# Five buffers instead of two for staged weights, and squares counted by section, in a two-layer attention kernel

## The chip, the cores and the metric

The kernel runs on one core of one Trainium2 chip. The metric is device time in microseconds (us) of that core; lower is better. The core's engines work side by side, each through its own list of instructions in a fixed order: PE multiplies matrices (PEld is its weight load), DVE, ACT and POOL do elementwise work, and SP issues the DMA transfers. An instruction that waits holds everything behind it on its own engine. An engine's order is not the order of the text: the build plans it, and may put an instruction ahead of others that stand before it in the text when what it needs is expected to be there.

## What is computed

A trunk of two layers on x of 1024 rows and 1024 columns, all float32. Each layer computes

```
x <- x + W_out( mixer(RMSNorm(x)) * silu(z) )
```

where q, k, v and z of the mixer come from one combined input projection of the normed x, and a last RMSNorm follows. Layer 0's mixer is "FoX", causal attention of 16 heads of 64 with a forget gate:

```python
logits = jnp.einsum('bqhd,bkhd->bhqk', q[:, s0:s1], k[:, :s1]) * scale
logits = logits + c[:, :, s0:s1, None] - c[:, :, None, :s1]     # c: running sum of log forget gates
logits = jnp.where(tk[None, :] <= tq[:, None], logits, NEG)
p = jax.nn.softmax(logits, axis=-1)
outs.append(jnp.einsum('bhqk,bkhd->bqhd', p, v[:, :s1]))
```

Layer 1's mixer is "NSA": 16 query heads in 4 groups attend in three ways, to 63 compressed blocks of keys, to 8 chosen blocks of 64 keys, and to a window of 512 keys; the three results are summed with sigmoid gates. The projections of both layers, and both output projections, are what the weights of this case are for.

## The kernel before, in words

**Weights come in sections.** The columns of the input projections are cut into sections of 128 columns, each 1024 x 128 float32, 512 KB in DRAM and 4 KB in each of the 128 partitions of on-chip memory. FoX has 32 of them (k, v, q and z for each of 8 pairs of heads, `p`), NSA has 28 (kc, vc, qa, qr, v, ka, kr, z). Rows of W_out, 8 for each layer, are brought in the same shape so that their sum of squares is known in advance; they are called `wor`.

**Life of a section.** `Staged` (L163) takes a place of the tag `wst`, of which there are two, and issues the transfer on SP (L169). `square` (L172) sums the squares of the section on ACT (L176, into `wj`, the sum in `wsq`) and `total` copies the sum for the next step on ACT (L133, `wsb`, three places). `split` (L180) spreads the sum over the partitions with a small matmul on PE (L138, `wsum`), makes a power of two of it on DVE, and writes the section as two float16 halves, `whi` on DVE (L190) and `wlo` in four pieces on POOL (L193 and L194). With the last `wlo` piece the section's `wst` place is free. A `wor` has no split: its place is free after its square.

**How far ahead.** `next_w` (L347 for FoX, L929 for NSA) is called where a section begins. It keeps two sections split, so the next one is split while this one is used, and then `stage_next` begins the transfer of the one after that, if none is staged. The squares wait in a list; `flush` (L159) runs all of them, and `project` (L213), the loop of 24 matmuls of one half of a section, calls it after its fifth step. `wo_square` (L366) stages one `wor` beside each pair of heads in FoX, and beside eight of NSA's sections.

**What runs beside it.** `merge` weaves two streams: for FoX the attention of head pairs (`FoxDuo`, scores, softmax and the product with v) with the projections of the next pair (`fox_fill`); for NSA first the compressed attention (`cmp_main`), then the attention of the 32 head halves (`NsaSuper`), with projections and the output projection as filling. Around a section's use ACT and DVE also copy its product out: K (L433, L434), v (L508, L509), Q (L530, L531) and z (L85, L86).

**Others with the same tag.** `OutPart` (L578) loads parts of the attention output into a `wst` place for the output projection, and `load_wout` (L678) loads W_out rows through `wst` places and converts them (L695 to L700). Both are in the stretch in which a layer's output projection runs. `load_wout` with `half` set first adds up the `wor` squares.

Of the kernel before, what the change touches and what calls it, by code (L numbers as in the profile page):

```python
# [8 lines left out]
F32 = mybir.dt.float32  # L9
# [12 lines left out]
P = 128  # L22
H = 16
HD = 64
KC = D // P
# [16 lines left out]
def tile_fox_nsa(ctx, tc, a, out):  # L42
# [36 lines left out]
    wp = ctx.enter_context(tc.tile_pool(name="wp", bufs=2))  # L79
# [8 lines left out]
    class Norm:  # L88


        def __init__(self, pool, x, name, bufs):
            self.x, self.n = x, 0
            self.st = pool.tile([P, 4], F32, tag="st", bufs=bufs, name=f"st_{name}")
            self.h = pool.tile([P, D], F32, tag="h", bufs=bufs, name=f"h_{name}")
# [19 lines left out]
    def to_hT(h, t, hT, name, ps=(ps_t, ps_t)):  # L114
        for c in range(2):
            pt = ps[c](f"pth_{name}_{c}")
            for j in range(4):
                T.transpose(pt[:, j * P:(j + 1) * P], h[:, (4 * c + j) * P:(4 * c + j + 1) * P], ident)
            hi = hT[t // 4][0][:, 4 * c:4 * c + 4, t % 4 * P:(t % 4 + 1) * P]
            lo = hT[t // 4][1][:, 4 * c:4 * c + 4, t % 4 * P:(t % 4 + 1) * P]  # L120
            v = pt.rearrange("p (k t) -> p k t", k=4)
            A.copy(hi, v)
            V.tensor_tensor(lo, v, hi, OP.subtract)
# [7 lines left out]
    def total(sq, name, ps):  # L131
        sb = wp.tile([P, 2], BF16, tag="wsb", bufs=3, name=f"wsb_{name}")
        A.copy(sb, sq.to_broadcast([P, 2]))  # L133
        return lambda: spread(sb, name, ps)
# [21 lines left out]
    gains = []  # L156
    squares = []

    def flush():  # L159
        while squares:  # L160
            squares.pop(0)()

    class Staged:  # L163


        def __init__(self, src, name, acc=None):
            self.name, self.acc, self.sq = name, acc, None
            self.st = wp.tile([P, KC, P], F32, tag="wst", bufs=2, name=f"wst_{name}")
            dma(self.st, src)  # L169
            squares.append(self.square)  # L170

        def square(self):  # L172
            if self.sq is None:
# [23 lines left out]
    def weight_scale(pt, u, undo):  # L197

        b, e, r, x = (u[:, i:i + 1] for i in range(4))
        exponent(pt, r, b)  # L200
        V.tensor_scalar(r, r, 2.0 ** 77, None, OP.mult)
        if undo is None:
            V.tensor_scalar(e, b, 2.0 ** 50, None, OP.mult)
        else:
            V.tensor_scalar(e, b, undo, 2.0 ** 50, OP.mult, OP.mult)
        return e, r, x
# [6 lines left out]
    def project(w, hT, half, pt):  # L213
        for k in range(KC):
            mm3(pt, w[0][:, k, :], w[1][:, k, :], hT[half][0][:, k, :], hT[half][1][:, k, :], k == 0, k == KC - 1)
            if k == 4:
                flush()
            yield 650
# [121 lines left out]
    st = tc.alloc_tile_pool(name="start", bufs=1, side="right")  # L340
# [3 lines left out]
    fox_order = [x for p in range(8) for x in ((1, p), (2, p), (0, p), (3, p))][1:]  # L344
    wq, staged = [], []

    def next_w():  # L347
        while len(wq) < 2 and (staged or fox_order):
            if not staged:
                stage_next()  # L350
            wq.append(staged.pop(0).split(gains[0].undo))
        stage_next()
        return wq.pop(0)

    def stage_next():
        if not staged and fox_order:
            kind, p = fox_order.pop(0)
            staged.append(Staged(a["fox_w"][kind * 8 + p], f"{'qkvz'[kind]}{p}"))

# [3 lines left out]
    def w_row(i, k):  # L363
        return w_out[i][k * P:(k + 1) * P, :].rearrange("p (k c) -> p k c", k=KC)
# [75 lines left out]
    def opening():  # L440
        gB = st.tile([P, D], F32, name="gB")
        xs = []
        for i in range(2):
            gains.append(Gain(a["norm_g_c"][:, i * KC:(i + 1) * KC], i))
        for t in range(NT):
            xs.append(st.tile([P, D], F32, tag="x", bufs=7, name=f"x_{t}"))
            dma(xs[t], a["x"][t * P:(t + 1) * P, :])
            if t == 0:
                dma(gB, a["norm_g"][0:1, :].to_broadcast([P, D]))
            if t == 1:  # L450
                k0w = Staged(a["fox_w"][8], "k0")
            if t == 3:
                dma(wfst, a["fox_w_f"].rearrange("(k p) c -> p k c", p=P))
                dma(bf[32:32 + H], a["fox_b_f"].rearrange("o h -> h o"))
                dma(below, a["below"])
        dma(tri, a["tri"])
        side = []
        hs = {}
        with tc.manual_schedule(engines={T.engine, V.engine, A.engine}):
            for t in range(NT + 1):  # L460
                if t < NT:
                    nm = Norm(st, xs[t], f"n0_{t}", 3)
                    nm.square(slice(0, D))
                    hs[t] = nm.finish(gB, gain=gains[0])
                if t:
                    to_hT(hs.pop(t - 1), t - 1, hT, f"n0_{t - 1}", (ps_s, ps_t))
                if t == 2:
                    flush()
                if t == 3:
                    wq.append(k0w.split(gains[0].undo))  # L470
                    A.activation(fj, wfst, AF.Square, accum_out=fsq)
                    fsum = total(fsq, "f", ps_t)
                if t == 4:
                    e, r, _ = weight_scale(fsum(), fu, gains[0].undo)
                    wfe.append(e)
                    V.tensor_scalar(wf[:, :, 0:H], wfst, r, None, OP.mult)
                    V.scalar_tensor_tensor(wf[:, :, 32:32 + H], wfst, r, wf[:, :, 0:H], OP.mult, OP.subtract)
                    side = [k0] * 9 + [gate0] * 8
                if t >= 5:
                    for g in side[0:5]:  # L480
                        next(g)
                    del side[0:5]
            for g in side:
                next(g)

    k0, gate0 = fox_k(0), forget_gate()
    opening()

    def v_transposes(vt, half, vT, name):
# [88 lines left out]
    class OutPart:  # L578


        def __init__(self, i, t, k0, stop):
            self.name, self.i, self.t, self.k0, self.stop = f"{i}_{t}_{k0}", i, t, k0, stop
            self.of = wp.tile([P, KC, P], F32, tag="wst", bufs=2, name=f"of{self.name}")[:, k0:stop, :]
            dma(self.of, oF[k0 * P:stop * P, t * P:(t + 1) * P].rearrange("(k p) t -> p k t", p=P))

        def square(self):
# [91 lines left out]
    def load_wout(pool, i, half):  # L678

        if half:  # L680
            u = consts.tile([P, 6], F32, name=f"wou{i}")
            V.tensor_reduce(u[:, 4:5], sqW[i], AX.X, OP.add)
            wout_undo[i], r, _ = weight_scale(total(u[:, 4:5], f"wo{i}", ps_t)(), u, None)
            wout_scale[i] = r
        r = wout_scale[i]
        hi, lo = (pool.tile([P, 4, D], F16, tag=f"h{half}{x}", name=f"wo{i}_{half}_{x}") for x in range(2))
        yield 0
        for k in range(4):
            st = wp.tile([P, KC, P], F32, tag="wst", bufs=2, name=f"wor{i}_{half}_{k}")
            dma(st, w_row(i, 4 * (1 - half) + k))  # L690
            st = st.rearrange("p k c -> p (k c)")
            for c in range(2):
                yield 400 if i else 200
                cs = slice(c * 512, c * 512 + 512)
                A.activation(hi[:, k, cs], st[:, cs], AF.Copy, scale=r)  # L695
                if c:
                    V.scalar_tensor_tensor(lo[:, k, cs], st[:, cs], r, hi[:, k, cs], OP.mult, OP.subtract)
                else:
                    G.tensor_scalar(st[:, cs], st[:, cs], r, 1.0, OP.mult, OP.mult)
                    G.tensor_tensor(lo[:, k, cs], st[:, cs], hi[:, k, cs], OP.subtract)  # L700
        ready.setdefault("wout", []).append((hi, lo))
# [220 lines left out]
    nq, wq, squared = list(nsa_w), [], list(range(KC))  # L922

    def stage_next():
        if not staged and nq:
            kind, i = nq.pop(0)
            staged.append(((kind, i), Staged(a["nsa_w"][nsa_i[kind] + i], f"n{kind}{i}")))

    def next_w(key):  # L929
        while len(wq) < 2 and (staged or nq):  # L930
            stage_next()
            k, st = staged.pop(0)
            wq.append((k, st.split(gains[1].undo)))
        stage_next()
        k, w = wq.pop(0)
        assert k == key
        return w
# [222 lines left out]
    gwe, r, _ = weight_scale(total(gu[:, 4:5], "g", ps_t)(), gu, gains[1].undo)  # L1160
# [550 lines left out]
```

## Time and profile before

| | |
|---|---|
| three runs | 1683.37, 1693.61, 1690.54 us; median 1690.54 us |
| the profiled execution | 1687.15 us, of which the span of the instructions is 1685.4 us |
| instructions | 30876 |
| DMA | 237.44 MB in 406558 packets, 141 GB/s on average |
| DVE busy | 1126.5 us, 67% of the span |
| POOL busy | 734.6 us, 44% of the span |
| squares of staged weights (L176) | 76 on ACT, 1.06 us each, with a read of the sum of 0.19 us |
| transfers of staged weights (L169) | 76, in FoX from 3.5 us to 547.6 us, in NSA from 691.8 us to 1327.7 us |

Read in time, the span has these stages: the opening, in which x is normed (0 to about 62 us); FoX (62 to about 580 us); the end of layer 0 with its output projection and the norm for layer 1 (580 to about 750 us); NSA's projections and compressed attention (750 to about 1140 us); NSA's attention with the z projections as filling (1140 to about 1605 us); the end. The profile counts an engine as idle before an instruction and names what ended the idle time; PEclk is the granted clock of PE as a share of full speed.

### The profile page before, as it was taken

What the parts mean: (1) busy time and instruction counts of PE and PEld (TensorE: products, weight loads), DVE (VectorE), ACT (ScalarE), POOL (GpSimd) and SP (SyncE); (2) the same over time, 40 slices, a digit from 0 to 9 for tenths busy, and PEclk for the clock granted to TensorE, in tenths of its full rate; (3) what the DMA queues carried; (4) which work ended last, traced back from release to release, by engine and by line L of the source; (5) the groups of instructions that cost most, each with busy time, mean ns of one, the idle gap of its engine ahead of it and who ended that gap; (6) DMA issues with size and microseconds to landing.
All of it is one profiled execution on the core that took longest, in us unless ns stands there. A gap on an engine that the chain in (4) does not pass through costs nothing. (4 is left out here: it accounts for less than half of the span.)

```text
span 1685.4 us, 30876 instructions
## 1 busy us (share of the span) xinstructions
PE 1425.8 (85%) x10581; PEld 840.7 (50%) x10581; DVE 1126.5 (67%) x3223; ACT 943.1 (56%) x2353; POOL 734.6 (44%) x1057
## 2 busy tenths in 40 slices
PE   5898988988788877958988787887999999989887
PEld 3344444444344433434534444445777777857633
DVE  6486677785767778383724355856787788868754
ACT  6375556655555556254323356656676667766642
POOL 1354334344334431023533334535666676765600
PEclk9899999999899997969989999999999999999999
DMA  6355566766566677251343447756678686776632
GB/s 213 92 137 135 136 134 139 160 124 146 115 136 126 169 169 141 69 186 50 112 129 112 153 125 177 177 167 165 143 143 161 135 189 152 163 172 147 125 111 100
DMA packets 406558, 237.44 MB, mean 141 GB/s; under 512 B 332352, under 2 KB 356544, under 8 KB 406400
## 3 DMA queue, kind: packets, MB, share of 16 engines
q1 hardware_dynamic: 406400, 235.47, 58.2%
q8 instruction: 83, 1.36, 0.4%
q14 instruction: 75, 0.61, 0.1%
HBM read 120.32 MB, written 35.19 MB: 92 GB/s over the span
## 5 line engine op out<-in xcount | busy, mean ns | idle before, releaser
L1481 ACT ACTIVATE P_n<-P_n,m_n 128x640 f32<-128x640 f32 (+7 forms) x256 | 186.7, 730 | 50.7 <-DVE m_n L1480 26.2
L1471 PE MATMUL S_n<-nk,nq 128*128 128x320 f32 (+5 forms) x768 | 194.5, 367 | 13.7 <-DVE m_n L1478 11.9
L782 ACT ACTIVATE P<-P,m 128x512 f32<-128x512 f32 (+1 forms) x192 | 116.4, 607 | 83.9 <-DVE m L773 83.8
L784 DVE SCALAR_TENSOR_TENSOR hl<-P,hl 128x512 f16<-128x512 f32 (+1 forms) x192 | 116.6, 623 | 48.4 <-ACT hl L783 47.3
L1485 POOL TENSOR_TENSOR hl_n<-P_n,hl_n 128x640 f16<-128x640 f32 (+4 forms) x128 | 141.9, 1109 | 8.9
L1471 PEld LDWEIGHTS S_n<-nk,nq 128*128 128x128 f32 x768 | 127.4, 194 | 32.6 <-DVE m_n L1478 18.4
L1484 POOL CAST hl_n<-P_n 128x640 f16<-128x640 f32 (+4 forms) x128 | 76.8, 600 | 130.9 <-ACT P_n L1481 127.9
L753 POOL TENSOR_TENSOR Bd<-B,tri 128x128 f32<-128x128 f32 x128 | 62.7, 504 | 155.8 <-DVE m L773 147.2
L229 DVE SCALAR_TENSOR_TENSOR ptl_n<-ptp_n,pth_n 128x512 f16<-128x512 f32 (+1 forms) x160 | 100.2, 633 | 38.5 <-ACT pth_n L228 37.0
L1478 DVE CUSTOM_DVE_ANT_0 P_n<-S_n,wmask 128x640 f32<-128x640 f32 (+2 forms) x192 | 112.8, 595 | 17.1 <-PE S_n L1471 14.0
L228 ACT ACTIVATE pth_n<-ptp_n 128x512 f16<-128x512 f32 (+1 forms) x160 | 86.1, 544 | 40.7 <-PE ptp_n L1503 38.6
L209 PE MATMUL y<-wo,ohi 128*128 128x512 f16 x230 | 90.4, 393 | 11.8 <-ACT ohi L598 9.2
L1503 PE MATMUL ptp_n<-ident,P_n 128*128 128x128 f32 x576 | 92.1, 281 | 8.5 <-DVE ptl_n L229 4.3
L764 PE MATMUL S<-K,Q 128*128 128x512 f16 (+1 forms) x192 | 62.3, 342 | 42.3 <-DVE m L773 26.9
L783 ACT ACTIVATE hl<-P 128x512 f16<-128x512 f32 (+1 forms) x192 | 92.2, 511 | 4.7 <-DMA pT<-hl 3.3
L211 PE MATMUL y<-wo,olo 128*128 128x512 f16 x230 | 88.6, 389 | 1.4 <-DVE olo L599 1.2
L210 PE MATMUL y<-wo,ohi 128*128 128x512 f16 x230 | 89.7, 390 | 0.0
L1511 PE MATMUL O_n<-nv,pth_n 128*128 128x64 f16 x576 | 71.8, 195 | 13.9 <-ACT pth_n L228 13.9
L1503 PEld LDWEIGHTS ptp_n<-ident,P_n 128*128 128x128 f32 x576 | 66.7, 142 | 25.7 <-DVE ptl_n L229 12.5
L1478 DVE CUSTOM_DVE_ANT_0 P_n<-S_n,bias 128x640 f32<-128x640 f32 (+1 forms) x64 | 65.1, 1018 | 12.4 <-PE S_n L1471 12.0
L798 PE MATMUL O<-v,pT 128*128 128x128 f16 x576 | 60.2, 224 | 13.6 <-DMA pT<-hl 12.1
L1512 PE MATMUL O_n<-nv,pth_n 128*128 128x64 f16 x576 | 71.2, 194 | 0.0
(557 smaller groups left out, 4659.9 us busy)
## 6 DMA issues: line engine op xcount, KB each, us to landing
nq<-qD SPq DMA_DIRECT2D x64, 256.0 KB
B<-cD SPq DMA_DIRECT2D x16, 512.0 KB
nq<-qD SPq DMA_DIRECT2D x64, 128.0 KB
x<-in_x_dram SPq DMA_DIRECT2D x8, 512.0 KB
wst_k<-in_fox_w_dram SPq DMA_DIRECT2D x8, 512.0 KB
wst_v<-in_fox_w_dram SPq DMA_DIRECT2D x8, 512.0 KB
xr<-in_x_dram SPq DMA_DIRECT2D x8, 512.0 KB
wst_q<-in_fox_w_dram SPq DMA_DIRECT2D x8, 512.0 KB
```

The lines of the kernel that those rows point to most:

```text
L209: T.matmul(ps, wh, mh, start=first, stop=False, **kw)
L210: T.matmul(ps, wh, ml, start=False, stop=False, **kw)
L211: T.matmul(ps, wl, mh, start=False, stop=last, **kw)
L229: V.scalar_tensor_tensor(lo[:, 0:n], pt[:, 0:n], scale, h, OP.mult, OP.subtract)
L782: A.activation(L[:, 0:n], L[:, 0:n], AF.Exp, bias=init, scale=-1.0, accum_out=self.lr[:, col + c:col + c + 1])
L783: A.activation(hi[:, cs], L[:, 0:n], AF.Copy, scale=UP)
L784: V.scalar_tensor_tensor(lo[:, cs], L[:, 0:n], UP, hi[:, cs], OP.mult, OP.subtract)
L1471: T.matmul(ps[:, b, 0:w], self.q[x][:, qi * P:(qi + 1) * P], k[:, k0 + b * w:k0 + b * w + w], start=(x == 0), stop=(x == 1))
L1478: V.tensor_tensor_reduce(dst, src, mk, 1.0, 3e38, OP.add, OP.min, m)
L1481: A.activation(L, L, AF.Exp, bias=m, scale=-1.0, accum_out=self.l[:, y, qi:qi + 1])
L1485: G.tensor_tensor(hl[:, n:2 * n], L, hl[:, 0:n], OP.subtract)
L1503: T.transpose(pt[:, (x + i) * P:(x + i + 1) * P], L[:, kb * P - k0:(kb + 1) * P - k0], ident)
```

## The change

The tag `wst` gets five places instead of two wherever it is used. `next_w` now keeps two sections staged behind the two split ones, so that in the text a section's transfer is issued three sections before its use and not two. Each entry in the list of squares carries the number of the section in which it was staged (`now`), and `flush` runs those that are at least one section old; a new call `flush(0)` in `load_wout` and the one in the opening run all. For a section the square stands at the same place of the text as before, while its transfer stands one section earlier. A `wor` of NSA has its square one section later in the text than before.

```diff
+    now = [0]
+
+    def flush(age=1):
+        while squares and squares[0][0] + age <= now[0]:
+            squares.pop(0)[1]()
-    def flush():
-        while squares:
-            squares.pop(0)()
...
-            self.st = wp.tile([P, KC, P], F32, tag="wst", bufs=2, name=f"wst_{name}")
+            self.st = wp.tile([P, KC, P], F32, tag="wst", bufs=5, name=f"wst_{name}")
             dma(self.st, src)
-            squares.append(self.square)
+            squares.append((now[0], self.square))
...
     def next_w():
+        now[0] += 1
         while len(wq) < 2 and (staged or fox_order):
             if not staged:
                 stage_next()
             wq.append(staged.pop(0).split(gains[0].undo))
-        stage_next()
+        while len(staged) < 2 and fox_order:
+            stage_next()
         return wq.pop(0)
 
     def stage_next():
-        if not staged and fox_order:
+        if fox_order:
...
                 if t == 2:
-                    flush()
+                    flush(0)
...
-            self.of = wp.tile([P, KC, P], F32, tag="wst", bufs=2, name=f"of{self.name}")[:, k0:stop, :]
+            self.of = wp.tile([P, KC, P], F32, tag="wst", bufs=5, name=f"of{self.name}")[:, k0:stop, :]
...
     def load_wout(pool, i, half):
 
         if half:
+            flush(0)
...
-            st = wp.tile([P, KC, P], F32, tag="wst", bufs=2, name=f"wor{i}_{half}_{k}")
+            st = wp.tile([P, KC, P], F32, tag="wst", bufs=5, name=f"wor{i}_{half}_{k}")
...
     def stage_next():
-        if not staged and nq:
+        if nq:
...
     def next_w(key):
+        now[0] += 1
         while len(wq) < 2 and (staged or nq):
-            stage_next()
+            if not staged:
+                stage_next()
             k, st = staged.pop(0)
             wq.append((k, st.split(gains[1].undo)))
-        stage_next()
+        while len(staged) < 2 and nq:
+            stage_next()
```

## The prediction

> **What bounds the kernel now.** I first read the clock and the busy times: on average PE bounds the kernel, and ACT, which has the squares, is busy about half of the time.
>
> ```profile
> core 0: 1685.4 us, clock 0.938
> PE 1425.8 (85%) x10581; PEld 840.7 (50%) x10581; DVE 1126.5 (67%) x3223; ACT 943.1 (56%) x2353; POOL 734.6 (44%) x1057
> ```
>
> A share over the whole span says little, so next the table by stage (length, then busy time of PE, PEld, DVE, ACT, POOL, then the granted clock). These are FoX and the start of NSA.
>
> ```profile
> core 0: us, PE busy (x) PEld busy (x) DVE busy (x) ACT busy (x) POOL busy (x), PEclk, DMA share, GB/s
> 62.00:580.00 518.00, 442.81 (x2774) 221.74 (x2772) 364.69 (x1192) 296.22 (x725) 219.15 (x364) 0.95 0.61 138
> 690.00:780.00 90.00, 71.76 (x319) 35.32 (x317) 51.46 (x112) 37.58 (x88) 19.57 (x32) 0.81 0.35 116
> ```
>
> In FoX PE is idle for 518 - 443 = 75 us, and no other engine is near full. So I asked for what ACT waits in FoX; the list names ACT's line, what ended the wait, the sum, the count and the longest.
>
> ```profile
> ACT wj_z L176 <- DMA wst_z<-in_fox_w_dram: 36.8, 8, 7.1
> ACT wj_v L176 <- DMA wst_v<-in_fox_w_dram: 34.1, 7, 6.8
> ACT wj_wor L176 <- DMA wst_wor<-in_fox_w_out_dram: 17.3, 6, 6.4
> ACT wj_k L176 <- DMA wst_k<-in_fox_w_dram: 11.1, 5, 3.6
> ACT wj_q L176 <- DMA wst_q<-in_fox_w_dram: 11.0, 5, 3.5
> ```
>
> That is 110.3 us in 31 waits, 3.6 us each, for a transfer that the square is to read. One of them in the timeline, engine by engine (start, length, and in brackets the idle time before):
>
> ```profile
> 143.65 1.74 POOL L194 TENSOR_TENSOR wlo_z<-wst_z,whi_z 128x256 f16<-128x256 f32 x2
> ...
> 145.42 0.33 SPq L169 DMA_DIRECT2D wst_v<-in_fox_w_dram  x1
> ...
> 148.95 1.06 ACT L176 ACTIVATE wj_v<-wst_v 128x1024 bf16<-128x1024 f32 x1 [6.44 <-DMA wst_v<-in_fox_w_dram]
> ...
> 150.74 0.68 DVE L531 SCALAR_TENSOR_TENSOR Q<-q,Q 64x512 f16<-64x512 f32 x1 [5.87 <-ACT Q L530]
> ...
> 151.48 0.61 PE L764 MATMUL S<-K,Q 128*128 128x512 f16 x1 [7.17 <-DVE Q L531]
> ```
>
> POOL's last piece of section z ends at 145.39 and frees a place; SP issues v's transfer 0.03 us later; it lands 3.5 us later; ACT, held by the square, copies Q only after it; PE, which needs Q, stood idle for 7.17 us. I found ten PE gaps of 2.9 us or more like this in FoX, each overlapping or right behind a wait of ACT for a square. One windows view has a window for each gap, and another the stretch of low clock that follows it; the first, the one above and the sums:
>
> ```profile
> 82.33:86.94 4.61, 0.00 (x1) 0.01 (x1) 0.68 (x1) 1.96 (x5) 1.48 (x2) 0.92 0.52 203
> 144.31:151.48 7.17, 0.00 (x0) 0.00 (x1) 1.24 (x2) 1.84 (x5) 5.43 (x10) 0.73 0.37 89
> sum 45.45, PE 0.02 PEld 0.01 DVE 14.82 ACT 25.03 POOL 10.03; mean PE 0.00 PEld 0.00 DVE 1.48 ACT 2.50 POOL 1.00
> 147.60:154.40 6.80, 2.92 (x9) 1.25 (x10) 2.35 (x7) 2.41 (x5) 2.14 (x4) 0.50 0.36 119
> sum 51.20, PE 41.15 PEld 16.96 DVE 36.91 ACT 32.24 POOL 14.69; mean PE 4.11 PEld 1.70 DVE 3.69 ACT 3.22 POOL 1.47
> ```
>
> So the waits cost FoX 45.45 us of idle PE and, as PE was busy for 41.15 us at a clock of 0.50, another 41.15 / 2 = 20.6 us: 66 us for 110.3 us of ACT's waits, 0.6 us of PE for each.
>
> The Trainium skill, page "TensorE: Matmul & The Clock Gate", Part 1 (the HAM clock gate), says that for modeling the ramp penalty is under 1% of a typical kernel's span, which by an estimate of mine from that sentence would be at most 17 us here for the whole kernel. The trace disagrees: the mean clock of 0.938 is 6% below full, so I keep the term of 20.6 us.
>
> **Why I do not expect FoX to get this back.** The question is what sets the moment of a transfer. By the text it is `next_w`. The transfers' own queue says otherwise:
>
> ```profile
> 13.81 0.42 SPq L169 DMA_DIRECT2D wst_v<-in_fox_w_dram  x1
> 14.28 0.46 SPq L668 DMA_DIRECT2D xr<-in_x_dram  x1
> 28.31 0.33 SPq L169 DMA_DIRECT2D wst_q<-in_fox_w_dram  x1
> ```
>
> L668 loads x for the output projection at the very end of layer 0, some 600 us later, and is issued at 14.28 us: the planned order takes a transfer as soon as it has a place, wherever it stands in the text. The same holds for the sections. The waits of SP in FoX:
>
> ```profile
> SPq L169 <- POOL wlo_k L194: 34.1, 7, 9.1
> SPq L169 <- POOL wlo_v L194: 29.5, 7, 6.3
> ```
>
> So a section's transfer is already held by its place and not by its place in the text. With five places the queue runs five deep instead of two, but in the steady state each `wlo` that ends still lets exactly one transfer go, at the same moment as now, only for a section three places further on. And a square is planned like that too: at 148.95 us v's square stands ahead of the Q copies of the section before, which come earlier in the text. If the plan again puts each square on ACT where it expects the transfer to have landed, ACT meets the same 3.5 us after the same late `wlo`. What changes for certain is that no section is late any more for its own `split`.
>
> **The change, part by part.**
>
> *Removed: PE's own waits for a section that is not there.* NSA uses sections faster, and a `wor` stands between them. There PE itself waits in `split`; one case, then PE's waits for `wsum` from 690 to 1140 us, then the two stretches of low clock behind the two long ones:
>
> ```profile
> 957.61 0.33 SPq L169 DMA_DIRECT2D wst_wor<-in_nsa_w_out_dram  x1
> 962.51 0.33 SPq L169 DMA_DIRECT2D wst_nv<-in_nsa_w_dram  x1
> ...
> 967.72 1.06 ACT L176 ACTIVATE wj_nv<-wst_nv 128x1024 bf16<-128x1024 f32 x1 [4.12 <-DMA wst_nv<-in_nsa_w_dram]
> 968.90 0.19 ACT L133 CAST wsb_nv<-wsq_nv 128x2 bf16<-128x2 f32 x1
> 969.14 0.16 PE L138 MATMUL wsum_nv<-wsb_nv,ones 128*128 128x2 bf16 x1 [7.26 <-ACT wsb_nv L133]
> PE wsum_nv L138 <- ACT wsb_nv L133: 7.3, 1, 7.3
> PE wsum_nz L138 <- DVE ptl_c L226: 6.4, 1, 6.4
> PE wsum_nka L138 <- ACT wsb_nka L133: 1.6, 1, 1.6
> sum 13.60, PE 8.27 PEld 3.42 DVE 8.80 ACT 4.58 POOL 3.78; mean PE 4.13 PEld 1.71 DVE 4.40 ACT 2.29 POOL 1.89
> ```
>
> With sections landed three places ahead these go: 7.3 + 6.4 + 1.6 = 15.3 us, and 8.27 / 2 = 4.1 us of clock: 19.4 us. Next in line there is the chain of the compressed attention, whose price I do not know; it can keep all of it (0).
>
> *Removed: waits of the output projections for their places.* `OutPart` and `load_wout` share the tag:
>
> ```profile
> ACT oj L590 <- DMA of<-oF: 23.9, 13, 4.3
> PE y L209 <- ACT ohi L598: 9.2, 6, 2.7
> ```
>
> PE waits 9.2 us for the halves behind those loads. The loads also wait for `oF`, which no place helps. I take half, 4.6 us, between 0 and 9.2.
>
> *Moved: transfers.* 76 transfers and 76 squares stay, with the same bytes. In the opening q, z and the next k can now go at about 14 us beside v. Each takes SP 0.33 us and lands in some 3.5 us (145.42 to 148.95); between 14.74 and 28.31 us SP issues nothing, which hides them. Were it not so, three of them would cost 10.5 us there. On SP a transfer that waits for its place holds the transposes behind it as it does now, by the same `wlo`, so I cost that at nothing; at worst, were the 64 us of the two rows above doubled, PE would pay by its own rate below.
>
> *Moved: squares.* In FoX zero, by the argument above. The ends: a gain of the whole 66 us, and a loss that the last rival prices. I take zero because the nearest row, the issue 0.03 us behind a `wlo`, is the steady state of the change as well.
>
> *Added: 12 KB in each partition* (three places of 4 KB), which shifts what is laid out behind it. No row shows a wait of that kind; the turn from FoX to NSA is where it could lie, with 90 - 71.76 = 18 us of idle PE. I take 0; a new wait there could cost that much again, and a better fit could spare as much, so 18 us to either side.
>
> The bookkeeping of `flush` and `now` is done at build time and costs nothing. Sum: 19.4 + 4.6 = 24 us. From the profiled execution's 1687.15 us that is **1663 us**. The median of the three runs is 1690.54, 3 us above that execution; I state the time against the execution.
>
> **The rivals.**
>
> *A. ACT's waits go (1613 us).* If the plan puts the squares later than the landing, because ACT has other work ready, FoX gains. For it: ACT is 56% busy, and a square may now be anywhere in four sections. Against it: where ACT is idle nothing holds a square back, and that is 222 us of FoX. Of each of the ten gaps about 1 us would stay (the copies take that): 45.45 - 10 = 35 us; three quarters of the clock's 20.6 us: 15. A quarter of these 50 us is lost to DVE, at 364.69 of 518 us the next engine: 38 us. NSA's largest group of such waits:
>
> ```profile
> ACT wj_wor L176 <- DMA wst_wor<-in_nsa_w_out_dram: 51.1, 8, 9.6
> ```
>
> At 0.6 that is 31 us, of which 19 are in my sum already: 12 more. 1663 - 38 - 12 = 1613.
>
> *B. Nothing changes (1687 us).* PE's waits for `wsum` give way to the chain of compressed attention, and the output projection waits for `oF`. The step would do what it says to the transfers, and nothing to the time.
>
> *C. Slower: the copy of the sum holds ACT (1717 us).* A square that runs three sections early is followed on ACT by the copy into `wsb` (L133), of which there are three places; the copy for one section must wait until PE has used the `wsum` of the third before it. Today it takes 0.19 us and waits for nothing; the nearest wait on ACT is the 3.6 us for a transfer. If each of the 60 sections (32 and 28) held ACT for 1.5 us more, between the two, PE would lose 60 x 1.5 x 0.6 = 54 us: 1663 + 54 = 1717. It decides from 24 / 0.6 / 60 = 0.7 us a section for a loss at all, and (24 + 17) / 0.6 / 60 = 1.1 us for a loss of 1%. For it: the plan hurries all it can. Against it: PE is the slowest engine in FoX, and ACT waiting for PE is mostly harmless.
>
> **How the numbers follow.** My forecast 0.50, A 0.20, B 0.15, C 0.15. About 1%, 17 us, is what a measurement of this kernel can tell from no change. The forecast's own range is 1645 (18 us better by the layout) to 1685 (both terms gone, or the layout against it); some 0.33 of its 0.50 lies below 1670. With nearly all of A and 0.02 of B that is 0.54 for faster. C without a fifth, and 0.03 of the others, is 0.15 for slower, and 0.31 remain for within 1%. The range reaches to A's time and into C: 1612 to 1705 leaves out half of A and most of C, 2 in 10.
>
> **What would show it.** Right: the transfers of L169 in FoX still start within 0.1 us behind a `wlo` of POOL, for a section further on; ACT's waits for squares in FoX stay above 80 us of 110.3; the ten gaps of PE do not shrink by more than a third; PE's waits for `wsum_nv` and `wsum_nz` are gone. Wrong, toward A: ACT's waits on L176 fall below 50 us in FoX, and its clock rises above 0.97. Wrong, toward C: a row in which ACT's L133 waits for PE's L138 with tens of us. What would break the forecast is a plan that orders ACT otherwise in FoX: the whole argument hangs on the square being put where its transfer is expected.

## The result: 1633 us, and where 56 us went

The kernel after takes 1632.99 us (median of four runs, 1628.07 to 1636.4), the kernel before in the same comparison 1688.72 us (median of four, 1683.37 to 1693.61). The ratio is 0.9668, with a 95% interval of 0.9626 to 0.9711: 3.3% faster. The prediction, 1663 us, has the direction, and the time lies in its whole range (1612 to 1705, which reaches to rival A), but not in the forecast's own (1645 to 1685): the gain is 56 us where it had 24.

The profile of the kernel after. First the span and clock, and the line of busy times (the profiled execution's own time is 1630.43 us):

```profile
core 0: 1628.7 us, clock 0.941
PE 1412.4 (87%) x10581; PEld 838.5 (51%) x10581; DVE 1130.5 (69%) x3223; ACT 939.9 (58%) x2353; POOL 736.4 (45%) x1057
```

The clock has hardly moved, and PE does the same 10581 matmuls. What ACT waits for in FoX (the list of waits, 62 to 580 us; sum, count and longest in us; L178 is the square's line now):

```profile
ACT wj_k L178 <- DMA wst_k<-in_fox_w_dram: 29.1, 6, 8.2
ACT wj_q L178 <- DMA wst_q<-in_fox_w_dram: 26.4, 6, 6.9
ACT wj_v L178 <- DMA wst_v<-in_fox_w_dram: 13.3, 5, 4.0
ACT wj_z L178 <- DMA wst_z<-in_fox_w_dram: 12.5, 6, 4.2
ACT wj_wor L178 <- DMA wst_wor<-in_fox_w_out_dram: 8.6, 5, 3.2
```

That is 89.9 us in 28 waits; before it was 110.3 in 31. So the waits are still there, at other sections. One of them in the timeline of the kernel after, to be laid beside the one that the prediction shows:

```profile
135.50 1.74 POOL L196 TENSOR_TENSOR wlo_z<-wst_z,whi_z 128x256 f16<-128x256 f32 x2
...
137.27 0.33 SPq L171 DMA_DIRECT2D wst_k<-in_fox_w_dram  x1
...
140.78 1.06 ACT L178 ACTIVATE wj_k<-wst_k 128x1024 bf16<-128x1024 f32 x1 [6.42 <-DMA wst_k<-in_fox_w_dram]
...
142.57 0.69 DVE L535 SCALAR_TENSOR_TENSOR Q<-q,Q 64x512 f16<-64x512 f32 x1 [5.86 <-ACT Q L534]
...
143.31 0.61 PE L769 MATMUL S<-K,Q 128*128 128x512 f16 x1 [6.97 <-DVE Q L535]
```

It is the same chain, link by link: z's last `wlo` ends at 137.24, a transfer goes 0.03 us later, ACT's square waits 6.42 us for it, the copy of Q and with it PE wait behind the square. Only the section has changed, v there and k here.

Where the time comes from is best read at places that both kernels pass. The table gives when PE starts or ends there, from the timelines of both traces:

| PE | before | after | earlier by |
|---|---|---|---|
| first score matmul `S` of FoX | 86.94 | 78.41 | 8.5 |
| first matmul of section k6 | 441.82 | 428.28 | 13.5 |
| first matmul of section z7, the last of FoX | 558.88 | 534.37 | 24.5 |
| end of the last `S` of FoX | 665.76 | 632.11 | 33.7 |
| first score matmul `S_n` of NSA | 1137.43 | 1103.40 | 34.0 |
| end of the last `S_n` | 1592.76 | 1539.43 | 53.3 |
| end of the span | 1685.37 | 1628.65 | 56.7 |

The steady part of FoX, from the first `S` to k6, gives 5 us in 350, and everything between FoX's last score and NSA's first, some 471 us that include the stretch where the prediction looked for 19.4 us, gives 0.4. The gain is in the opening (8.5), at the end of FoX with the output projection beside it (20 from k6 on), and in NSA's attention (19); the end of the kernel gives the last 3.4.

The same stretches with what ACT waits for in them, from the lists of waits of both traces. "Squares" are ACT's idle times that end with the transfer that a square is to read, "output" those that end with a load of the output projection (`of` or `wor`); both in us, before and then after:

| stretch | length | squares | output |
|---|---|---|---|
| start to first `S` | 86.9, 78.4 | 18.2, 8.0 | 0, 0 |
| first `S` to k6 | 354.9, 349.9 | 67.7, 74.4 | 0, 0 |
| k6 to last `S` | 223.9, 203.8 | 28.4, 12.8 | 23.1, 11.2 |
| last `S` to first `S_n` | 471.7, 471.3 | 146.1, 122.7 | 0, 0 |
| first `S_n` to last `S_n` | 455.3, 436.0 | 15.6, 3.7 | 16.7, 10.4 |
| last `S_n` to the end | 92.6, 89.2 | 0, 0 | 5.7, 6.5 |

In the steady part of FoX the waits did not fall at all. At the start and the ends of the streams, where the time fell most, the waits for squares fell, and at the ends those for the output projection's loads with them. The attention stage as a window of its own, first before, then after (length; busy time of PE, PEld, DVE, ACT, POOL; clock):

```profile
1137.43:1592.76 455.33, 413.88 (x4889) 322.75 (x4889) 353.17 (x1002) 316.31 (x753) 303.90 (x375) 0.98 0.73 155
```

```profile
1103.40:1539.43 436.03, 408.95 (x4889) 320.67 (x4889) 352.95 (x1002) 313.89 (x746) 304.01 (x375) 0.98 0.75 160
```

The work is the same 4889 matmuls, in 19.3 us less. SP's transfers before and after show what has moved, here the first and last of the four nz sections that still arrived during attention before, and the last one after:

```profile
1168.70 0.34 SPq L169 DMA_DIRECT2D wst_nz<-in_nsa_w_dram  x1
...
1327.74 0.35 SPq L169 DMA_DIRECT2D wst_nz<-in_nsa_w_dram  x1
```

```profile
1134.43 0.52 SPq L171 DMA_DIRECT2D wst_nz<-in_nsa_w_dram  x1
```

The queue now runs three places further ahead, so each stream of weights ends earlier, and what lies behind its last square is free of such waits: NSA's last section is on its way at 1134 us and not at 1328, and of the nz squares two instead of five fall into attention. FoX's stream ends the same way, its last transfer at 476.17 us where it was at 547.65. The waits of PE for `wsum` and for the output projection's halves after (the list of waits):

```profile
PE wsum_nz L138 <- DVE ptl_c L228: 7.2, 1, 7.2
...
PE y L211 <- ACT ohi L602: 4.3, 4, 2.1
```

`wsum_nv` and `wsum_nka` are gone, `wsum_nz` has stayed. Its timeline:

```profile
1077.86 0.36 SPq L171 DMA_DIRECT2D wst_nz<-in_nsa_w_dram  x1
...
1082.32 1.06 ACT L178 ACTIVATE wj_nz<-wst_nz 128x1024 bf16<-128x1024 f32 x1 [7.92 <-DMA wst_nz<-in_nsa_w_dram]
...
1089.38 0.16 PE L138 MATMUL wsum_nz<-wsb_nz,ones 128*128 128x2 bf16 x1 [7.16 <-DVE ptl_c L228]
```

The section whose sum this matmul spreads, the second of the nz, had landed long ago (its transfer went at 1015.94); ACT, which had to finish the compressed attention's tiles before DVE could write `ptl_c`, stood for 7.92 us in front of the square of a later section, whose transfer had been let go at 1077.86. The kernel before shows the same chain:

```profile
1112.04 0.34 SPq L169 DMA_DIRECT2D wst_nz<-in_nsa_w_dram  x1
...
1116.32 1.06 ACT L176 ACTIVATE wj_nz<-wst_nz 128x1024 bf16<-128x1024 f32 x1 [7.85 <-DMA wst_nz<-in_nsa_w_dram]
...
1123.39 0.16 PE L138 MATMUL wsum_nz<-wsb_nz,ones 128*128 128x2 bf16 x1 [6.41 <-DVE ptl_c L226]
```

There too it is the second nz, whose square had run at 1102.90, and ACT stands in front of the square of the third. So `wsum_nz` was never a wait for its own section: it is the early square of another, in both kernels.

### The profile page after: what moved, and what is told of

The parts are those of the page before. It is cut to its first block, busy times and chain, and to the rows that moved or that the text cites. A ratio compares the mean times of both kernels' runs of the same rounds, so it can differ in the third digit from the quotient of the medians.

```text
span 1628.7 us, 30853 instructions
## 1 busy us (share of the span) xinstructions
PE 1412.4 (87%) x10581; PEld 838.5 (51%) x10581; DVE 1130.5 (69%) x3223; ACT 939.9 (58%) x2353; POOL 736.4 (45%) x1057
## 3 DMA queue, kind: packets, MB, share of 16 engines
q8 instruction: 83, 1.36, 0.4%
## 5 line engine op out<-in xcount | busy, mean ns | idle before, releaser
L1486 DVE CUSTOM_DVE_ANT_0 P_n<-S_n,wmask 128x640 f32<-128x640 f32 (+2 forms) x192 | 113.1, 595 | 19.3 <-PE S_n L1479 16.6
L211 PE MATMUL y<-wo,ohi 128*128 128x512 f16 x230 | 89.8, 390 | 6.5 <-ACT ohi L602 4.3
```

The source lines that it names most:

```text
L211: T.matmul(ps, wh, mh, start=first, stop=False, **kw)
L1486: V.tensor_tensor_reduce(dst, src, mk, 1.0, 3e38, OP.add, OP.min, m)
```

## The experiments

All are timed against the kernel before on the same chip; a ratio is to that. In the sums below, "ACT's waits" are ACT's idle times that end with the transfer that a square of a staged section is to read, over the whole span: 276.2 us in the kernel before (110.4 in FoX, 146.1 from there to NSA's first `S_n`, 15.6 in NSA's attention), 221.5 in the kernel after (89.8, 122.7 and 3.7). The rest, 4.1 and 5.3 us, lies ahead of FoX.

**The parts of the change: places alone, text alone.**

```diff
 e1: the kernel before, at all three places of the tag
-tag="wst", bufs=2
+tag="wst", bufs=5
 e2: the kernel after, at all three places of the tag
-tag="wst", bufs=5
+tag="wst", bufs=2
```

> The kernel before with five places for wst instead of two and nothing else: transfers are begun two sections ahead in the text, squares as before. Theory P (a transfer goes when a place comes free, whatever the text says): the same as the changed kernel, 1625 to 1641 us, transfers of L169 still 0.03 us behind a wlo. Rival T (the third section ahead and the age of the squares matter): at most half of the gain, 1655 us or more.

> The changed kernel with two places for wst instead of five: three sections ahead in the text, squares by age. Theory P: as the kernel before, 1680 to 1700 us. Rival T: 1670 us or less.

Places alone: 1630.08 us, ratio 0.9662 (0.9628 to 0.9695), ACT's waits 211.8 us. Text alone: 1691.70 us, ratio 1.0035 (1.001 to 1.0059), ACT's waits 282.2 us. The places are the whole gain. The third section in the text and the age of a square gain nothing; with two places they are 0.35% slower. That fits an order that takes a transfer when it has a place and a square when it expects the transfer to have landed, wherever the text has them.

**The number of places.**

```diff
 e5 and e12: the kernel after, at all three places of the tag
-tag="wst", bufs=5
+tag="wst", bufs=3    (e12: 4)
```

> The changed kernel with three places in place of five. If the gain comes from the ends of the streams (each place more lets the last transfers and their squares fall one section earlier) and from the opening, then the opening's 8 us come whole with the third place, and of the remaining 48 us one third: 1688 - 8 - 16 = 1664, between 1655 and 1672. If it comes only when a stream's end is wholly free of squares, three places give the opening alone: 1680. If the third place is all that is needed: 1632. In all cases ACT still waits over 200 us for transfers before its squares.

> The changed kernel with four places. With three, z's transfer still went at 28.34 us and the first S stood at 85.14 us; with five z's goes at 14.9 us and the first S stands at 78.41. If the opening hangs on the place for z, the fourth place brings z's transfer to about 15 us and the first S to 78 to 80 us; with half of the rest between three places (1667) and five (1633) the time is about 1647 (1640 to 1655). If the opening needs the fifth place (for k1), the first S stays above 84 us and the time is 1650 to 1660.

Three: 1667.20 us, ratio 0.9867 (0.9828 to 0.9906). Four: 1639.53 us, ratio 0.9706 (0.9654 to 0.9759). So 1689, 1667, 1640 and 1633 us for two to five places. Three came out at the time expected, but for another reason in part: of the opening's 8.5 us only 1.8 came with the third place. SP's queue in the opening, with three places and then with four:

```profile
14.43 0.53 SPq L171 DMA_DIRECT2D wst_q<-in_fox_w_dram  x1
28.34 0.33 SPq L171 DMA_DIRECT2D wst_z<-in_fox_w_dram  x1
```

```profile
14.56 0.53 SPq L171 DMA_DIRECT2D wst_q<-in_fox_w_dram  x1
15.13 0.44 SPq L171 DMA_DIRECT2D wst_z<-in_fox_w_dram  x1
```

With three, q goes early and z goes only at 28.34; the first `S` stands at 85.14 us. With four, z goes at 15.13 and the first `S` stands at 80.55 (78.41 with five). That looks as if the opening hung on z's place, but two other runs speak against it: in e2, with two places, z goes at 58.16 and the first `S` still stands at 80.69, and in e11 below, with three, at 28.33 and 79.05. What goes with the first `S` is how often ACT waits for a transfer in front of a square between 60 us and that `S`. The last such wait in the run with three places, and then in e2:

```profile
82.37 1.06 ACT L178 ACTIVATE wj_q<-wst_q 128x1024 bf16<-128x1024 f32 x1 [4.82 <-DMA wst_q<-in_fox_w_dram]
...
85.14 0.61 PE L769 MATMUL S<-K,Q 128*128 128x512 f16 x1 [4.33 <-DVE Q L535]
```

```profile
78.15 1.06 ACT L178 ACTIVATE wj_wor<-wst_wor 128x1024 bf16<-128x1024 f32 x1 [4.17 <-DMA wst_wor<-in_fox_w_out_dram]
...
80.69 0.39 PE L769 MATMUL S<-K,Q 128*128 128x512 f16 x1 [1.53 <-DVE Q L535]
```

| run | places | z's transfer | waits from 60 us on: count, sum | first `S` |
|---|---|---|---|---|
| before | 2 | 60.97 | 4, 14.2 | 86.94 |
| e5 | 3 | 28.34 | 4, 13.8 | 85.14 |
| e2 | 2 | 58.16 | 3, 10.9 | 80.69 |
| e12 | 4 | 15.13 | 3, 11.0 | 80.55 |
| e11 | 3 | 28.33 | 2, 6.6 | 79.05 |
| after | 5 | 14.92 | 2, 6.7 | 78.41 |

So the opening, too, seems to be a matter of early squares in front of the copies of Q. The table shows that the two go together; no run moves one of these squares alone, and where v0's square is itself held late (e3 below) the first `S` is late without such waits. The rest grows with each place: the end of the span comes 26, 46 and 57 us earlier with three, four and five.

**The last squares of each stream.**

```diff
 e10: the kernel before
-                A.activation(j, self.st..., AF.Square, accum_out=self.sq)
+                i = A.activation(j, self.st..., AF.Square, accum_out=self.sq)
+                if self.name in ("k7", "v7", "q7", "z7", "wor0_7", "nz4", "nz5", "nz6", "nz7"):
+                    tc.keep_in_program_order(i)
```

`keep_in_program_order` puts the square on ACT behind the ACT instruction that stands before it in the text; the planned order may no longer draw it forward.

> The kernel before, two places, in which only the squares of the last sections (k7, v7, q7, z7 and the last row of fox_w_out, then nz4 to nz7) are held behind the ACT instruction before them in the text. In the kernel before, ACT waits 35.5 us in all in front of these nine, and the change moves just these to earlier times. If the gain at the ends of the streams is that of these nine waits, 35.5 x 0.6 = 21 us go (1660 to 1675), about half of them by the last S of FoX and half within the attention of NSA. If the ends gain by something else, the time stays within 8 us of that before.

1663.94 us, ratio 0.9841 (0.9814 to 0.9867): 25 us from nine squares, with two places. In the kernel before, the four of NSA stand like this on ACT (first and last):

```profile
1173.20 1.06 ACT L176 ACTIVATE wj_nz<-wst_nz 128x1024 bf16<-128x1024 f32 x1 [3.19 <-DMA wst_nz<-in_nsa_w_dram]
...
1331.66 1.06 ACT L176 ACTIVATE wj_nz<-wst_nz 128x1024 bf16<-128x1024 f32 x1 [4.33 <-DMA wst_nz<-in_nsa_w_dram]
```

Held back, none of the four has a wait in front of it. The attention stage of e10 as a window:

```profile
1132.26:1570.57 438.31, 408.79 (x4889) 321.44 (x4889) 353.31 (x1002) 316.28 (x753) 303.39 (x375) 0.98 0.76 161
```

438.31 us, 17.0 less than before, with the same 753 instructions on ACT; the change gave 19.3. So four waits of 15.6 us together are worth 17 us there: in this stage a us of waiting on ACT costs about a us, not 0.6. In FoX the five squares brought z7 forward by 7.2 us, of which 4.2 remain at the last `S`: from k6 on ACT waits 16.3 us less for squares, but 5.9 us more (29.0 for 23.1) for the loads of the output projection.

**The output projections' places.**

```diff
 e9: the kernel before, in OutPart and in load_wout
-tag="wst", bufs=2
+tag="wso", bufs=3
```

> The kernel before, with three places of their own for the loads of the output projections (OutPart and load_wout); the staged sections keep their two. Memory is that of the change. If the places that the output projections got are the source of the gain at the end of FoX and at the end of the kernel, 15 to 30 us of the 56 appear here: 1660 to 1673, with the last S of FoX 10 us or more earlier. If that gain belongs to the staged sections, which end earlier in their stream, the time is 1680 to 1690 and the sections of FoX stand where they stood.

1677.33 us, ratio 0.9942 (0.9917 to 0.9966): 11.7 us, between the two expectations. The last `S` of FoX comes 3.1 us earlier, the end of the kernel 11.8; 9.5 of these arise after the 672nd of NSA's 768 `S_n` matmuls, where the second output projection runs. NSA's attention stage alone is 7.4 us shorter. What fell most is ACT's wait for W_out rows, by 11.0 us; in front of `OutPart`'s loads it fell from 23.9 to 18.3. Its waits in front of the conversion of W_out rows (L695), before and then in e9:

```profile
ACT wo L695 <- DMA wor<-in_fox_w_out_dram: 11.8, 5, 5.6
ACT wo L695 <- DMA wor<-in_nsa_w_out_dram: 9.9, 5, 4.2
```

```profile
ACT wo L695 <- DMA wor<-in_fox_w_out_dram: 5.6, 4, 2.5
ACT wo L695 <- DMA wor<-in_nsa_w_out_dram: 5.1, 3, 2.9
```

They are halved; with the change 6.2 of 21.7 us are left. In NSA's attention e9's 7.4 us and e10's 17.0 are more than the 19.3 of the change, so the two cannot simply be added there.

**Squares held in the order of the text.** The waits that the change leaves go when the squares are no longer drawn forward. The condition in the code below holds while `ready` has entries, which is from the first head pair on and again once NSA has its first ones; the squares written ahead of that stay free.

```diff
 e3: the kernel after; e4: the kernel before; e8: the kernel before with five places
-                A.activation(j, self.st..., AF.Square, accum_out=self.sq)
+                i = A.activation(j, self.st..., AF.Square, accum_out=self.sq)
+                if len(gains) == 2 and ready:
+                    tc.keep_in_program_order(i)
 e6: as e3, and e11: as e6 with three places
-                if len(gains) == 2 and ready:
+                if len(gains) == 2 and ready and self.name not in ("v0", "q0", "z0", "k1"):
 e7: as e3, and in Staged.__init__
-            dma(self.st, src)
+            i = dma(self.st, src)
+            if len(gains) == 2 and ready:
+                tc.keep_in_program_order(i)
```

> The changed kernel with each square on ACT held behind the ACT instruction that stands before it in the text, from the first head pair on. Data and work are the same. Theory P (ACT's 221 us of waits stay because the square stands on ACT where its transfer was expected, and they cost PE time in the steady part): ACT's waits for squares fall below 40 us, the ten gaps of FoX shrink, and the time falls by 30 us or more, to 1560 to 1603 us. Rival S (the waits lie in slack, and only the ends of the streams count): 1625 to 1641 us, with ACT's waits gone all the same. Rival L (a square in text order is too late for its split): over 1641 us, with PE waiting for wsum.

> The kernel before (two places) with the squares held in text order in the same way. Theory P: the transfer goes at the same moment as before, half a section before the square, so a part of ACT's 276 us of waits goes, but splits get late: 1650 to 1690 us. Rival S: 1680 to 1700 us. If the order of the squares alone were all, it would reach the time of the changed kernel with squares held, under 1605 us.

> As e3_squares_pinned, but the squares of the sections v0, q0, z0 and k1 may be placed freely again. If the late opening of e3 (first S at 85.67 us where the changed kernel has 78.41) comes from the square of v0, which waited behind ACT's other work until 54.65 us, the first S comes back to 78 to 80 us and the time is about 1520 (1514 to 1524). If what is lost at the opening is made up later by a stage that waits for something else, the time stays at 1527.

> As e3_squares_pinned, with each transfer held on SP behind the SP instruction before it in the text as well. If only ACT's order mattered, the transfers still land long before their squares (30 to 60 us lie between in e3) and the time is 1520 to 1535. If SP's early transfers, which wait for a place with transposes behind them, cost something too, the time falls below 1515. If the text's place is too late for a transfer, ACT waits for squares again (over 30 us) and the time is above 1545.

> The kernel before with five places and with its squares held in the order of the text; the text still writes a transfer one section ahead and its square straight behind. If the distance in the text is what lets a pinned square find its section landed, ACT waits about as with two places (130 us) and the time is 1570 to 1595. If the places are enough, because a transfer goes early as soon as a place is free wherever the text has it, ACT's waits are under 20 us and the time is 1525 to 1540.

> As e6_first_four_free with three places in place of five. Two places with pinned squares left ACT waiting 130.6 us for transfers (1595 us), five left none (1523). If one place more is enough to let a transfer start a whole section before its square, ACT's waits fall below 30 us and the time is 1525 to 1545. If the time goes with the number of places, it is a third of the way: 1595 - 24 = 1571.

| run | places | time, us | ratio | ACT's waits, us |
|---|---|---|---|---|
| e4, old text | 2 | 1595.36 | 0.9459 (0.9428 to 0.949) | 130.6 |
| e11, first four free | 3 | 1540.62 | 0.9104 (0.9078 to 0.9131) | 40.7 |
| e8, old text | 5 | 1525.92 | 0.9032 (0.8994 to 0.9069) | 0 |
| e3 | 5 | 1527.08 | 0.9044 (0.8997 to 0.9091) | 0 |
| e7, transfers held too | 5 | 1535.78 | 0.9092 (0.9052 to 0.9132) | 22.3 |
| e6, first four free | 5 | 1522.72 | 0.9017 (0.8984 to 0.905) | 0 |

With five places and the squares alone held, no square waits for a transfer. A section of e6, its transfer on SP and its square on ACT:

```profile
135.28 0.33 SPq L171 DMA_DIRECT2D wst_z<-in_fox_w_dram  x1
...
170.69 1.04 ACT L178 ACTIVATE wj_z<-wst_z 128x1024 bf16<-128x1024 f32 x1
```

35 us lie between them where 3.5 lay before, and the square has no idle time in front of it. The page's line and the two stages of e6:

```profile
PE 1375.8 (90%) x10581; PEld 826.5 (54%) x10581; DVE 1129.8 (74%) x3223; ACT 941.9 (62%) x2353; POOL 739.1 (49%) x1057
```

```profile
62.00:580.00 518.00, 481.40 (x3183) 249.07 (x3182) 427.88 (x1386) 342.63 (x849) 246.57 (x393) 0.98 0.74 161
690.00:780.00 90.00, 84.90 (x434) 45.22 (x433) 54.34 (x114) 36.59 (x61) 41.39 (x64) 0.98 0.38 119
```

In the same 518 us PE runs 3183 matmuls, where the kernel before had 2774 and the kernel after 2880. The stretch from FoX's last `S` to NSA's first `S_n`, which the change left at 471 us, takes 417.0 us in e6: it was ACT's early squares that held it. e3 came out below its expected range: taken over the whole kernel, ACT's 276.2 us, in NSA as in FoX, were worth some 0.6 us each. Its late opening (v0's square at 54.65 us, first `S` at 85.67) is cured in e6, where v0's square runs at 24.88 and the first `S` starts at 79.86; e6 and e3 differ by 4 us, and their intervals overlap. Old text or new makes no difference here either (e8, e3). What does is the number of places: with two, 28 of the 76 squares still wait when they are held. Three give most of it. Holding the transfers in the order of the text as well gains nothing: e7 is 13 us behind e6, 7 of them in the opening (first `S` at 86.72), and nine squares wait again for transfers that now start later. The best version is e6, 1522.72 us, some 7% below the kernel after.

## Why the prediction was wrong in its size

The step that failed is "Moved: squares", with its value of zero, and the place from which it came, "the nearest row ... is the steady state of the change as well". That is so for the steady state, where ACT waits 74.4 us for squares after and 67.7 before, and it left out that a stream has a start and an end: at the start, from k6 to FoX's last `S` and in NSA's attention these waits fell from 62.2 to 24.5 us, and those stretches give 48 of the 56 us, with the output projections' share in them. Point by point:

- **The transfers' moment: right.** From 62 to 580 us 23 of 31 transfers of staged weights start within 0.1 us behind the end of a `wlo` of POOL, where 27 of 36 did before. SP's waits after, two of the rows:

```profile
SPq L171 <- POOL wlo_z L196: 26.8, 6, 6.8
SPq L171 <- POOL wlo_k L196: 24.9, 6, 5.7
```

- **ACT's waits in FoX: right in kind.** 89.9 us, above the 80 that were to stand. The gaps of PE of 2.9 us or more beside them fell from ten to six, from 45.45 us to 27.02, more than the third that I had allowed. Their sum in a windows view of the kernel after:

```profile
sum 27.02, PE 0.01 PEld 0.00 DVE 8.74 ACT 13.11 POOL 5.24; mean PE 0.00 PEld 0.00 DVE 1.46 ACT 2.19 POOL 0.87
```

- **The price of 0.6 us of PE's time for each us of ACT's waits: right as a mean, not stage by stage.** Against the kernel before, e3 took away 276.2 us of waits and 159 us of time: 0.58, which includes what the places give beside. e4 took away 145.6 and 91: 0.62. From the kernel after to e3, where only the order differs, it is 221.5 and some 105 us: 0.48. From before to e6 it is 0.71 from the first `S` to k6 (67.7 and 48.2 us) and 0.37 from the last `S` to the first `S_n` (146.1 and 54.7); in e10 it is about 1 in NSA's attention. I had used 0.6 for FoX alone.
- **"Removed: PE's own waits", 19.4 us: wrong.** The stretch from FoX's last score to NSA's first gained 0.4. Of the 15.3 us, only the 8.9 of `wsum_nv` and `wsum_nka` were waits for a section, and these went. The 6.4 of `wsum_nz` I had misread: its row names DVE's `ptl_c`, held up by an early square, and it has stayed, 7.2 us now. What is late next there are ACT's other early squares: of their 146.1 us of waits 122.7 are left, and with all of them gone the stretch is 54.7 us shorter (e6). Why the 23.4 us that did go gave only 0.4 stays open; with the places alone (e1) the stretch is 8.2 us shorter.
- **"Moved: transfers" in the opening, 0: wrong.** I listed that q, z and the next k would go early, asked only what they cost and not what waits for them. With these transfers early, ACT waits in front of two squares between 60 us and the first `S` and not four, and that `S` comes 8.5 us earlier. The gap of 4.61 us in front of it, first of the ten that were to stay, is 0.26 us now.
- **"Moved: squares", 0: wrong.** Over the whole span ACT's waits fell by 276.2 - 221.5 = 54.7 us; at 0.6 that is 33 us. In NSA's attention the case is shown singly: e10 gets 17.0 us there by four squares, where the change got 19.3.
- **"Removed: waits of the output projections for their places", 4.6 us: too small.** e9 gives 11.7. I had priced `OutPart`'s loads and not those of `load_wout`, in front of which ACT's waits fell most.
- **12 KB of memory, 0:** e9 has the same memory as the change and its sections of FoX stand within 2.5 us of where they stood, so no cost shows.
- **Rival A** named the right lever and the wrong means: ACT's waits do not go with more places, but with the order held. **Rival C** hardly occurs: in the kernel after, ACT's copy of a sum waits for a `wsum` of PE four times, 5.7 us in all, 1.36 of them before `wsb_nz` at 1089.58 us; in the kernel before it never does.

Summed anew: 33 for ACT's waits in front of squares and 12 for the output projections make 45 of the 56 us; the opening's 8.5 are no term of their own, since 10.2 of the 54.7 us of waits lie there. The 33 us are a rate times a sum, and they do not lie where the rate would put them: from the last `S` to the first `S_n` the waits fell by 23 us and the time hardly, in NSA's attention by 12 us and the time by 19. Of the 20 us from k6 to FoX's last `S`, e9 and e10 show 3.1 and 4.2 at the last `S`. Each takes away only one kind of wait there: in e9 ACT still waits 28.3 us for squares, in e10 29.0 us for the output projection's loads, where the change leaves 12.8 and 11.2. No run has both, so whether the other 13 us come from taking away the two together is not shown.

## What to carry to other kernels

Here transfers start the moment a buffer comes free, and more buffers hardly made each wait shorter (4.2 us on average before, 3.9 after): they moved the stream forward. So look for the gain at a stream's start and behind its end, and at everything else that uses the same buffers. When an in-order engine waits for a transfer with urgent work queued behind, look at what put the waiting instruction there; here one call that kept it in its place in the text gained 91 us with two places and some 105 on top of five, where the three places more had gained 56. Buffers and order belong together: order alone leaves half of the waits, buffers alone four fifths.

## What the runs showed of the hardware

ACT's waits, through the gaps that they leave on PE, go with a lower clock of PE. PE's 10581 matmuls take 1425.8 us in the kernel before and 1375.8 us in e6, with the mean granted clock at 0.938 and 0.964: 50 of some 164 us between the two spans are not idle time but the same matmuls in less busy time. By the two means of the clock 1425.8 us would become 1425.8 x 0.938 / 0.964 = 1387 us, so the clock accounts for some 39 of the 50 by this estimate; where the other 11 come from is not settled. The Trainium skill, page "TensorE: Matmul & The Clock Gate", Part 1, puts the ramp penalty at under 1% of a typical kernel span for modeling. That sentence stands beside the warm-up at a kernel's start, so it says nothing of a clock that falls again and again behind gaps, as here, and the prediction should not have held the two against each other. The 39 us are 39 / 1685 = 2.3% of the span.
